# A hybrid decoder step: the pooling stage with feature-major rows, one ordered load queue, a norm centred on four tiles, and activation rows of 272 floats

## The chip, the cores and the metric

One core of one Trainium2 chip. The metric is the device time of one execution in microseconds (us). Lower is better.

## What is computed

One step of a small decoder trunk, for a prompt (1 x 256 tokens) and a sample group (8 x 1 token) that share all weights; both stand side by side as 264 columns. The model width is 2048.

```python
# layer 0: pooling mixer; layer 1: gated linear attention (GLA)
for i in range(2):
    x = layer_norm(ALPHA * x + mixer_i(x), ...)
    x = layer_norm(ALPHA * x + sq_relu(x @ w1[i] + b1[i]) @ w2[i] + b2[i], ...)   # w1: 2048 x 8192

# pooling mixer, four groups of 512 channels, windows w = 2, 4, 8, 16
p = trailing_mean(x_group, w) - x_group          # samples: over 15 stored rows and the new one
y = concat_g(p_g @ w_group[g]) * pool_scale
```

The outputs are the two results y, the new pooling states (npp, nps: the last 15 input rows) and the new GLA states. All is float32.

## The kernel before, in words

Activations lie feature-major: a tile is 128 features x 264 columns, and x is 16 such tiles. Each big product is made in three passes, from a high part (`hh`, in the fp32r format) and a low part (`hl`) of x, and a high and a low part of the weight (`whi`, `wlo`): `mm3` issues hh x whi, hl x whi, hh x wlo. One **unit** is a weight block of 2048 x 128 (1 MB, `raw`): 48 matmuls into one bank `ps`. The whole program has 320 units: 128 for each MLP, 48 for the GLA inputs, 16 for the GLA output. `stage` loads a unit, casts its two halves on ACT (`whi`, L133) and subtracts on DVE (`wlo`, L134); `next_unit` stages two units ahead.

The halves of x are kept in `Parts`, two tiles to a pair: `[P, 2, NX]` with NX = 266 (264 columns and two for the norm's gain and bias). The second tile of a pair so starts 1064 bytes behind the first, and a pair takes 2128 bytes (the allocator gives it 2144).

The **pooling stage** comes first. `load(g)` brings a group's band matrix (the pooling weights over time), its input rows token-major (`xt`: two prompt halves and one tile of sample rows) and its weights (`pw`). `pooled(g, tiles)` makes for each tile the pooled rows px by four matmuls with the band (L755 to L758), turns the input to feature-major by three transposes (L764), and writes ALPHA * x to the residual tile `Z[m]` on ACT (L765, L766). `pool_products(g)` makes 16 plain float32 matmuls (L774), and `ln.add` adds each result to Z (L211).

`Norm` follows as tiles arrive. After the first 8 tiles it makes a provisional mean over them (`centre`, L224), and subtracts it from each tile (L232 in `shift`, L237 in `catch_up`). `gather` then makes the tile's hh and hl (L246, L247) and the sum of squares (L253, L255). So MLP units start before the norm is known: the two spare columns carry what corrects a product afterwards (`settle`, L322 to L324), and `stats` (the sums L266 to L273, then `rsqrt`) comes in the midst of unit 0.

PE's order is that of the program text. The orders of ACT, DVE, POOL and of the DMA queues are made by a scheduler when the program is built, and each engine then runs its own list strictly in that order.

Of the kernel before, what the change touches and what calls it, by code (L numbers as in the profile page):

```python
# [6 lines left out]
F32 = mybir.dt.float32  # L7
# [6 lines left out]
P = 128  # L14
# [4 lines left out]
N = NP + NS  # L19
NX = N + 2  # L20
DFF = 8192
NBLK = DFF // D
# [7 lines left out]
ALPHA = 4 ** 0.25  # L30
WARM = 18
PACE_A = (3, 3)
# [19 lines left out]
def _body(ctx, tc, nc, a, o, stop):  # L52
# [18 lines left out]
    ident = keep.tile([P, P], F32, name="ident")  # L71
    epst = keep.tile([P, 1], F32, name="epst")
    lnr = keep.tile([P, N], F32, name="lnr")
# [12 lines left out]
    class Parts:  # L86
# [93 lines left out]

    def rsqrt(out, v, y0, t):
        S.activation(y0, v, AF.Abs_reciprocal_sqrt, bias=epst)
        V.scalar_tensor_tensor(t, y0, -0.5, y0, ALU.mult, ALU.mult)
        V.scalar_tensor_tensor(t, v, EPS, t, ALU.add, ALU.mult)
        V.scalar_tensor_tensor(out, t, 1.5, y0, ALU.add, ALU.mult)
# [4 lines left out]
    class Norm:  # L190
        def __init__(self, name, x, ahead=1):
# [3 lines left out]
            self.shifted = 8  # L195
            self.n = 0
            self.met = 0
            self.done = 0
            self.sd, self.sq, self.c = lnm, lnq, lnr
            if x is not None:  # L200
                at = OFF[self.g]
                gb = par[:, at:at + 2 * KT].rearrange("p (c m) -> p m c", c=2)
                for m in range(0, KT, 2):
                    hi, lo = x.pair(m)
                    G.tensor_copy(hi[:, :, N:], gb[:, m:m + 2])
                    G.tensor_tensor(lo[:, :, N:], gb[:, m:m + 2], hi[:, :, N:].bitcast(F32), op=ALU.subtract)

        def add(self, ps, scale=1.0):
            m = self.n
            self.n += 1  # L210
            V.scalar_tensor_tensor(Z[m], ps[:, :N], scale, Z[m], ALU.mult, ALU.add)  # L211
            if m == 1:
                V.tensor_tensor(self.sd, Z[0], Z[1], op=ALU.add)
            elif 1 < m < 8:
                V.tensor_tensor(self.sd, self.sd, Z[m], op=ALU.add)
            if m == 7:
                later(1, self.centre)
            if m >= 8:
                self.gather(m)
                self.shift(m + 1 + self.ahead)  # L220

        def centre(self):
            cp = bank("ma")[:, :N]
            PE.matmul(cp, lhsT=ones, rhs=self.sd, start=True, stop=True)  # L224
            S.mul(self.c, cp, 1.0 / 1024)
            self.shift(8 + self.ahead)
            background.append(self.catch_up())
# [7 lines left out]
        def catch_up(self):  # L235
            for t in range(8):
                V.tensor_tensor(Z[t], Z[t], self.c, op=ALU.subtract)  # L237
                self.gather(t)
                yield
                if self.ahead:  # L240
                    yield

        def gather(self, t):
# [7 lines left out]
            else:  # L251
# [4 lines left out]
                else:  # L256
                    self.last = sq
            if t == 9:
                V.tensor_tensor(self.sd, Z[8], Z[9], op=ALU.add)
            elif 9 < t < KT - 1:  # L260
                V.tensor_tensor(self.sd, self.sd, Z[t], op=ALU.add)
# [7 lines left out]
        def close_sums(self):  # L269
            assert self.met == KT  # L270
            p1, p2 = self.p1, self.p2
            PE.matmul(p1, lhsT=ones, rhs=Z[KT - 1], start=False, stop=True)
            PE.matmul(p2, lhsT=ones, rhs=self.last, start=False, stop=True)  # L273
            t, v, y0 = wtile(), wtile(), wtile()
            S.activation(t, p1, AF.Square, scale=1.0 / D)
            S.mul(lnm, p1, 1.0 / D)
            V.scalar_tensor_tensor(v, p2, 1.0 / D, t, ALU.mult, ALU.subtract)
            rsqrt(lnr, v, y0, t)

# [78 lines left out]
    def gla(gctx, norm, xp, x, hg):  # L358
# [65 lines left out]
        class Head:  # L424
            def __init__(self, h):
# [294 lines left out]
        for h in range(HEADS):  # L720
            for t in range(4):
# [3 lines left out]
                if t == 0:  # L725
                    for e in range(2):
                        gated.fresh(2 * h + e, gp.tile([P, 2, NX], F32R, name="kq"[e] + "0") if h == 0 else None)
                heads[h].gate(t, ps, gated)
        assert not background and not pending
        return gated  # L730


    xs = Parts("a")
    with tc.tile_pool(name="poolp", bufs=2) as pp:
        band, xt = {}, {}

        pw, px = {}, {}

        def load(g):
            pw[g] = pp.tile([P, D], F32, name="pw", bufs=3)  # L740
            xt[g] = pp.tile([P, 3, 4 * P], F32, name="xt")
            band[g] = pp.tile([P, 280], F32, name="band")
            nc.sync.dma_start(band[g], a["band"][g])
            for t in range(4 if g == 0 else 1):
                c = slice(t * P, t * P + P) if g == 0 else slice(0, 4 * P)
                nc.sync.dma_start(xt[g][:, :, c], a["xt"][g][:, :, c])  # L746
            nc.sync.dma_start(pw[g], a["pw"][g])

        def pooled(g, tiles):
            x, w = xt[g], band[g]  # L750
            for t in tiles:
                c = slice(t * P, t * P + P)
# [12 lines left out]
                S.mul(Z[m][:, :NP], tp[:, :NP], ALPHA)  # L765
                S.mul(Z[m][:, NP:], tp[:, 3 * P - NS:3 * P], ALPHA)  # L766

        def pool_products(g):
            w = pw.pop(g)
            for mt in range(4):  # L770
# [4 lines left out]
                slot()  # L775
                ln.add(ps, prm("pool_scale", 4 * g + mt))

        S.preload_act_table(AF.Abs_reciprocal_sqrt)
        nc.sync.dma_start(ident, a["ident"])
        nc.scalar.dma_start(par, a["par"])  # L780
        V.memset(ones, 1.0)
        V.memset(epst, EPS)
        warm = bank("ma")
        for e in range(WARM):
            PE.matmul(warm[:, :P], lhsT=ones, rhs=ones, start=True, stop=True)
        load(0)
        load(1)
        pooled(0, range(4))
        ln = Norm("mix_0", xs, 0)
        for g in range(4):  # L790
            if g < 3:
                pooled(g + 1, (0,))
            pool_products(g)
            if g < 3:
                pooled(g + 1, (1,))
                slot()
                pooled(g + 1, (2, 3))
            if g < 2:
                load(g + 2)
            if g:  # L800
                stage()
    nc.gpsimd.dma_start(o["npp"], a["xtail"])
    nc.gpsimd.dma_start(o["nps"], a["nps_src"])

# [31 lines left out]
def layout(i):  # L836
# [4 lines left out]
    sp = i["state_pool"][0]  # L841
    rows = np.concatenate([xp, sp.reshape(NS * CTX, D), xs])
    r["xt"] = c(rows.reshape(3, P, 4, 4 * P).transpose(2, 1, 0, 3))
    band = np.zeros((4, P, 280), np.float32)
    for g, w in enumerate(WINDOWS):
# [6 lines left out]
        band[g, :, 144:272] = full[P:, P:]  # L852
        for b in range(NS):
            band[g, (b + 1) * CTX - (w - 1):(b + 1) * CTX, 272 + b] = np.float32(1.0 / w)
            band[g, NS * CTX + b, 272 + b] = np.float32(1.0 / w - 1.0)
    r["band"] = band
# [67 lines left out]
```

## Time and profile before

| | |
|---|---|
| time, median of 3 runs | 2081.34 us (2079.74 to 2082.94) |
| the profiled execution's own time | 2082.59 us |
| its span | 2080.8 us |
| mean granted TensorE clock | 0.995 |
| PE busy | 2055.9 us (99%), 16436 matmul records |
| DVE, ACT busy | 1254.3 us (60%), 1082.0 us (52%) |

The span is the time from the first to the last instruction in the profile; the time holds what lies around it (1.8 us here). PE is busy all but about 25 us. A matmul's end is modelled, and matmuls overlap, so busy time doesn't say how fast PE works: for that one counts matmuls over a stretch.

### The profile page before, as it was taken

What the parts mean: (1) busy time and instruction counts of PE and PEld (TensorE: products, weight loads), DVE (VectorE), ACT (ScalarE), POOL (GpSimd) and SP (SyncE); (2) the same over time, 40 slices, a digit from 0 to 9 for tenths busy, and PEclk for the clock granted to TensorE, in tenths of its full rate; (3) what the DMA queues carried; (4) which work ended last, traced back from release to release, by engine and by line L of the source; (5) the groups of instructions that cost most, each with busy time, mean ns of one, the idle gap of its engine ahead of it and who ended that gap; (6) DMA issues with size and microseconds to landing.
All of it is one profiled execution on the core that took longest, in us unless ns stands there. A gap on an engine that the chain in (4) does not pass through costs nothing.

```text
span 2080.8 us, 38806 instructions
## 1 busy us (share of the span) xinstructions
PE 2055.9 (99%) x16436; PEld 2018.4 (97%) x16436; DVE 1254.3 (60%) x1969; ACT 1082.0 (52%) x1650; POOL 54.9 (3%) x130
## 2 busy tenths in 40 slices
PE   8999999999999999999999999999999999999996
PEld 8999999999999999998899999999999999999996
DVE  3976444444444458986778758865444444444465
ACT  3657355345435545856656645566454345435543
POOL 0000000000000000011111010000000000000000
PEclk9999999999999999999999999999999999999998
DMA  6554555554455554477676444545555455554442
GB/s 239 193 186 175 175 180 183 183 177 175 177 182 183 182 175 171 153 253 256 237 267 237 161 172 175 178 171 180 182 183 180 174 176 180 183 182 177 174 177 83
DMA packets 67470, 386.19 MB, mean 186 GB/s; under 512 B 7808, under 2 KB 12160, under 8 KB 25808
## 3 DMA queue, kind: packets, MB, share of 16 engines
q1 hardware_dynamic: 61232, 363.28, 49.9%
q0 software_dynamic: 5920, 20.28, 2.6%
q8 instruction: 128, 2.10, 0.4%
q14 instruction: 46, 0.38, 0.1%
q10 hardware_dynamic: 144, 0.16, 0.0%
HBM read 362.65 MB, written 22.14 MB: 185 GB/s over the span
## 4 chain that ended last, share of the span: by engine, by line
PE 94%; DVE 3%; ACT 1%; DMA 1%; SPq 0%; issue 0%; ACTq 0%; DVEq 0%
PE ps L146 30%; PE ps L148 30%; PE ps L147 30%; PE ma L469 1%; DVE wlo L134 1%; PE mb L638 1%; PE ma L567 1%; DMA xt<-in_xt 0%; PE ps L774 0%; ACT whi L133 0%; PE mc L624 0%; DMA raw<-in_w 0%; PE ma L523 0%; SPq L746 0%; DMA s<-in_st 0%
## 5 line engine op out<-in xcount | busy, mean ns | idle before, releaser
L147 PE MATMUL ps<-hl,whi 128*128 128x264 f32 (+1 forms) x5120 | 1460.7, 285 | 0.0
L146 PE MATMUL ps<-hh,whi 128*128 128x264 f32 (+1 forms) x5056 | 1454.0, 288 | 0.0
L148 PE MATMUL ps<-hh,wlo 128*128 128x264 f32 (+1 forms) x5056 | 1443.1, 285 | 0.0
L134 DVE TENSOR_TENSOR wlo<-raw,whi 128x1024 fp32r<-128x1024 f32 x640 | 783.5, 1224 | 606.9 <-ACT whi L133 604.6
L133 ACT CAST whi<-raw 128x1024 fp32r<-128x1024 f32 x640 | 671.0, 1049 | 857.9 <-PE ps L147 832.6
L147 PEld LDWEIGHTS ps<-hl,whi 128*128 128x128 f32 x5120 | 968.7, 189 | 3.7 <-issue 1.4
L146 PEld LDWEIGHTS ps<-hh,whi 128*128 128x128 f32 x5056 | 953.7, 189 | 16.5 <-issue 15.8
L148 PEld LDWEIGHTS ps<-hh,wlo 128*128 128x128 f32 x5056 | 955.4, 189 | 0.0
L179 DVE TENSOR_TENSOR hl<-wt,hh 128x264 fp32r<-128x264 f32 x188 | 79.9, 431 | 15.5 <-ACT hh L178 9.8
L350 DVE TENSOR_TENSOR zt<-zt,ps 128x264 f32<-128x264 f32 x96 | 41.2, 429 | 65.7 <-PE ps L148 65.6
L178 ACT CAST hh<-wt 128x264 fp32r<-128x264 f32 x188 | 76.7, 410 | 7.4 <-DVE wt L661 3.2
L339 ACT ACTIVATE wt<-wt 128x264 f32<-128x264 f32 x128 | 54.4, 425 | 3.9
L627 DVE SCALAR_TENSOR_TENSOR s<-mc,k,s 128x512 f32<-128x512 f32 x64 | 45.8, 744 | 3.4 <-PE mc L624 3.4
L338 ACT ACTIVATE wt<-ps,par 128x264 f32<-128x264 f32 x96 | 45.6, 475 | 0.0
L211 DVE SCALAR_TENSOR_TENSOR zt<-ps,zt 128x264 f32<-128x264 f32 x48 | 20.7, 431 | 38.9 <-PE ps L148 38.9
L607 ACT ACTIVATE s<-s,sa 128x512 f32<-128x512 f32 x64 | 42.7, 713 | 2.6 <-DMA s<-in_st 2.6
L628 POOL DMA_DIRECT2D out_ngs<-s x64 | 34.7, 542 | 351.0 <-DVE s L627 343.3
L253 ACT ACTIVATE wt<-zt 128x264 f32<-128x264 f32 x60 | 23.4, 411 | 17.0 <-DVE zt L211 17.0
L774 PE MATMUL ps<-px,pw 128*128 128x264 f32 x128 | 30.9, 402 | 0.0
L774 PEld LDWEIGHTS ps<-px,pw 128*128 128x128 f32 x128 | 25.3, 200 | 4.4
L302 ACT ACTIVATE wt<-zt,par 128x264 f32<-128x264 f32 x48 | 27.4, 601 | 1.1 <-DVE zt L301 1.1
L246 ACT ACTIVATE hh<-zt,par 128x264 fp32r<-128x264 f32 x48 | 24.1, 511 | 5.6 <-DVE zt L237 3.6
(181 smaller groups left out, 897.3 us busy)
## 6 DMA issues: line engine op xcount, KB each, us to landing
raw<-in_w SPq DMA_DIRECT2D x256, 1024.0 KB, 4.8
raw<-in_win SPq DMA_DIRECT2D x48, 1024.0 KB, 5.0
s<-in_st SPq DMA_DIRECT2D x64, 256.0 KB, 5.5
out_ngs<-s POOLq DMA_DIRECT2D x64, 256.0 KB, 3.0
raw<-in_wout SPq DMA_DIRECT2D x16, 1024.0 KB, 4.8
pw<-in_pw SPq DMA_DIRECT2D x4, 1024.0 KB, 9.9
xt<-in_xt SPq DMA_DIRECT2D x3, 768.0 KB, 8.8
out_y<-zt SPq DMA_DIRECT2D x8, 264.0 KB, 2.2
```

The costliest lines, as they stand in the source:

```text
L133: S.copy(hi, src)
L134: V.tensor_tensor(lo, src, hi.bitcast(F32), op=ALU.subtract)
L146: PE.matmul(ps, lhsT=whi, rhs=xh, start=start, stop=False)
L147: PE.matmul(ps, lhsT=whi, rhs=xl, start=False, stop=False)
L148: PE.matmul(ps, lhsT=wlo, rhs=xh, start=False, stop=stop_)
L178: S.copy(x.hi[m][:, :N], src)
L179: V.tensor_tensor(x.lo[m][:, :N], src, x.hi[m][:, :N].bitcast(F32), op=ALU.subtract)
L338: S.activation(t, project(x)[:, :N], AF.Relu, bias=bias)
L339: S.activation(t, t, AF.Square)
L607: S.mul(s0s[b][hf], s0s[b][hf], sa[:, 2 * h + hf, b:b + 1])
L627: V.scalar_tensor_tensor(s0, vb, self.k[:, hf, NP + b:NP + b + 1], s0, ALU.mult, ALU.add)
L774: PE.matmul(ps[:, :N], lhsT=w[:, c], rhs=px[2 * g + k // 2][:, k % 2], start=k == 0, stop=k == 3)
```

## The change

- The prompt rows for the band matmuls come in one DMA per group (two for group 0), the sample rows in a new array `sw`, feature-major; the pooled sample columns are made on DVE (`sampled`) in place of matmuls. The residual rows come feature-major from a new array `xf` right into Z, in place of transposes and ACT copies. The residual is x and not ALPHA * x; pool_scale is divided by ALPHA (`psc`), and the norm's epsilon is halved (ALPHA squared is 2).
- All loads go on SP's queue, three groups at once at the start, `par` among them; `ident` comes later. The two state copies npp and nps go out in the first MLP unit, nps on SP's queue.
- `Norm` for this layer centres on 4 tiles (`first=4`) in place of 8. 18 warming matmuls become 10.
- Pairs of hh and hl are `[P, 2, 272]`: rows of 1088 bytes, pairs of 2176. The matmuls still read 264 or 266 columns.

```diff
+NROW = 272
-WARM = 18
+WARM = 10
...
             if th is None:
-                th = hslot(self.s, i, [P, 2, NX], F32R, "hh")
-            tl = hslot(self.s, 8 + i, [P, 2, NX], F32R, "hl")
+                th = hslot(self.s, i, [P, 2, NROW], F32R, "hh")
+            tl = hslot(self.s, 8 + i, [P, 2, NROW], F32R, "hl")
             self.pairs[i] = th, tl
             for e in range(2):
-                self.hi[2 * i + e], self.lo[2 * i + e] = th[:, e], tl[:, e]
+                self.hi[2 * i + e], self.lo[2 * i + e] = th[:, e, :NX], tl[:, e, :NX]
...
-            if m == 7:
+            if m == self.first - 1:
                 later(1, self.centre)
-            if m >= 8:
+            if m >= self.first:
                 self.gather(m)
                 self.shift(m + 1 + self.ahead)
...
+            if l == 0 and b == 0:
+                nc.gpsimd.dma_start(o["npp"], a["xtail"])
+                nc.sync.dma_start(o["nps"], a["nps_src"])
...
-                    self.k = gp.tile([P, 2, N], F32, name="k0")
-                    self.q = gp.tile([P, 2, N], F32, name="q0")
+                    self.k = gp.tile([P, 2, NROW], F32, name="k0")[:, :, :N]
+                    self.q = gp.tile([P, 2, NROW], F32, name="q0")[:, :, :N]
...
         def load(g):
             pw[g] = pp.tile([P, D], F32, name="pw", bufs=3)
-            xt[g] = pp.tile([P, 3, 4 * P], F32, name="xt")
-            band[g] = pp.tile([P, 280], F32, name="band")
+            xt[g] = pp.tile([P, 4, 2, P], F32, name="xt", bufs=3)
+            band[g] = pp.tile([P, 272], F32, name="band", bufs=3)
             nc.sync.dma_start(band[g], a["band"][g])
-            for t in range(4 if g == 0 else 1):
-                c = slice(t * P, t * P + P) if g == 0 else slice(0, 4 * P)
-                nc.sync.dma_start(xt[g][:, :, c], a["xt"][g][:, :, c])
+            if g == 0:
+                for t in range(0, 4, 2):
+                    nc.sync.dma_start(xt[g][:, t:t + 2], a["xt"][g][:, t:t + 2])
+                nc.sync.dma_start(sw, a["sw"])
+                nc.sync.dma_start(par, a["par"])
+            else:
+                nc.sync.dma_start(xt[g], a["xt"][g])
             nc.sync.dma_start(pw[g], a["pw"][g])
+            nc.sync.dma_start(ZT[:, 4 * g:4 * g + 4], a["xf"][g])
+
+        def sampled(g):
+            w = WINDOWS[g]
+            s = pp.tile([P, 4, NS], F32, name="ws")
+            if w == 2:
+                V.tensor_tensor(s, win[g][:, :, :, 0], win[g][:, :, :, 1], op=ALU.add)
+            else:
+                V.tensor_reduce(s, win[g], axis=mybir.AxisListType.X, op=ALU.add)
+            for i in range(2):
+                px[2 * g + i] = hslot("b", 2 * g + i, [P, 2, N], F32, "px")
+                V.scalar_tensor_tensor(px[2 * g + i][:, :, NP:], s[:, 2 * i:2 * i + 2], 1.0 / w,
+                                       win[g][:, 2 * i:2 * i + 2, :, w - 1], ALU.mult, ALU.subtract)
...
-                ps = bank("ma")[:, :N]
-                PE.matmul(ps[:, :P], lhsT=x[:, 0, c], rhs=w[:, :P], start=True, stop=True)
-                PE.matmul(ps[:, P:NP], lhsT=x[:, 1, c], rhs=w[:, 144:272], start=True, stop=False)
-                PE.matmul(ps[:, P:P + 16], lhsT=x[:, 0, c], rhs=w[:, P:144], start=False, stop=True)
-                PE.matmul(ps[:, NP:], lhsT=x[:, 2, c], rhs=w[:, 272:], start=True, stop=True)
-                if t % 2 == 0:
-                    px[m // 2] = hslot("b", m // 2, [P, 2, N], F32, "px")
-                S.copy(px[m // 2][:, t % 2], ps)
-                tp = bank("mb" if t % 2 else "mc")
-                for e in range(3):
-                    PE.transpose(tp[:, e * P:e * P + P], x[:, e, c], ident)
-                S.mul(Z[m][:, :NP], tp[:, :NP], ALPHA)
-                S.mul(Z[m][:, NP:], tp[:, 3 * P - NS:3 * P], ALPHA)
+                ps = bank("mb" if t % 2 else "mc")[:, :NP]
+                PE.matmul(ps[:, :144], lhsT=x[:, t, 0], rhs=w[:, :144], start=True, stop=False, skip_group_check=True)
+                PE.matmul(ps[:, P:], lhsT=x[:, t, 1], rhs=w[:, 144:], start=False, stop=True, skip_group_check=True)
+                S.copy(px[m // 2][:, t % 2, :NP], ps)
...
-        load(0)
-        load(1)
+        for g in range(3):
+            load(g)
+        sampled(0)
         pooled(0, range(4))
-        ln = Norm("mix_0", xs, 0)
+        V.tensor_scalar(psc, par[:, OFF["pool_scale"]:OFF["pool_scale"] + KT], 1.0 / ALPHA, None, ALU.mult)
+        ln = Norm("mix_0", xs, 0, half=True, first=4)
...
-            if g:
+            if g == 1:
+                nc.sync.dma_start(ident, a["ident"])
+            if g in (1, 2):
                 stage()
```

`pool_products` now also calls `pooled(g + 1, ...)` behind its second, third and fourth result. `stage` is called for two units in the pooling stage, where it was called for three; the third unit is staged when unit 0's product begins.

The scheduler's lists change with it. First ACT, around the first MLP units before: raw_702 is the weight of unit 2 (the third), wt_693 and wt_762 are the results of units 0 and 1 on their way to the MLP's inner activation.

```order
L133 CAST whi_704<-raw_702 128x1024
L246 ACTIVATE hh_100<-zt_85,par_78 128x264
L253 ACTIVATE wt_595<-zt_85 128x264
L275 ACTIVATE wt_657<-ma_651 128x264
L276 ACTIVATE lnm_83<-ma_651 128x264
L182 ACTIVATE wt_659<-wt_658,epst_81 128x264
L133 CAST whi_708<-raw_702 128x1024
L133 CAST whi_773<-raw_771 128x1024
L335 ACTIVATE wt_693<-wt_693,col_692 128x264
L339 ACTIVATE wt_693<-wt_693 128x264
L178 CAST hh_610<-wt_693 128x264
L133 CAST whi_777<-raw_771 128x1024
```

Unit 2's two casts, and the first of unit 3's, stand ahead of unit 0's result (L335).

ACT at the same place now: raw_501 is the weight of unit 2, raw_587 that of unit 3, wt_578 and wt_647 the results of units 0 and 1.

```order
L277 ACTIVATE wt_542<-ma_536 128x264
L278 ACTIVATE lnm_83<-ma_536 128x264
L183 ACTIVATE wt_544<-wt_543,epst_81 128x264
L337 ACTIVATE wt_578<-wt_578,col_577 128x264
L341 ACTIVATE wt_578<-wt_578 128x264
L179 CAST hh_485<-wt_578 128x264
L337 ACTIVATE wt_647<-wt_647,col_646 128x264
L341 ACTIVATE wt_647<-wt_647 128x264
L179 CAST hh_485<-wt_647 128x264
L134 CAST whi_503<-raw_501 128x1024
L134 CAST whi_507<-raw_501 128x1024
L134 CAST whi_589<-raw_587 128x1024
```

Unit 2's two casts now stand behind the result of unit 1 (its last row is the CAST of hh_485 from wt_647).

DVE at this place now, from the step that corrects unit 1's result (wt_647) to the low part of unit 2's weight (wlo_504). The rows L302 and L303 are the norm being applied to Z.

```order
L326 SCALAR_TENSOR_TENSOR wt_647<-lnm_83,col_646,wt_647 128x264
L303 TENSOR_TENSOR zt_85<-zt_85,lnm_83 128x264
L302 TENSOR_TENSOR zt_85<-zt_85,lnr_82 128x264 x2
L303 TENSOR_TENSOR zt_85<-zt_85,lnm_83 128x264 x2
L180 TENSOR_TENSOR hl_486<-wt_647,hh_485 128x264
L302 TENSOR_TENSOR zt_85<-zt_85,lnr_82 128x264 x2
L303 TENSOR_TENSOR zt_85<-zt_85,lnm_83 128x264 x2
L302 TENSOR_TENSOR zt_85<-zt_85,lnr_82 128x264 x2
L303 TENSOR_TENSOR zt_85<-zt_85,lnm_83 128x264 x2
L302 TENSOR_TENSOR zt_85<-zt_85,lnr_82 128x264 x2
L135 TENSOR_TENSOR wlo_504<-raw_501,whi_503 128x1024
```

Ten steps of L302 and L303 now stand between the low part of unit 1's result (L180) and unit 2's first `wlo`.

## Rows read from the trace of the kernel before

**Rows 1.** The page, parts 1 and 4: busy us, shares, and the last chain.

```profile
PE 2055.9 (99%) x16436; PEld 2018.4 (97%) x16436; DVE 1254.3 (60%) x1969; ACT 1082.0 (52%) x1650; POOL 54.9 (3%) x130
...
PE 94%; DVE 3%; ACT 1%; DMA 1%; SPq 0%; issue 0%; ACTq 0%; DVEq 0%
```

**Rows 2.** Groups by line and shape, PE, 161.6 to 822.4 us: count, busy, mean ns.

```profile
L146 PE MATMUL ps<-hh,whi 128*128 128x264 f32 x1792 | 511.3, 285 | 0.0
L148 PE MATMUL ps<-hh,wlo 128*128 128x264 f32 x1792 | 511.3, 285 | 0.0
L147 PE MATMUL ps<-hl,whi 128*128 128x264 f32 x1792 | 510.9, 285 | 0.0
```

**Rows 3.** Timeline, PE, unit of the first MLP: start us, length us, instruction.

```profile
397.58 0.28 PE L147 MATMUL ps<-hl,whi 128*128 128x264 f32 x1
397.70 0.28 PE L148 MATMUL ps<-hh,wlo 128*128 128x264 f32 x1
...
397.94 0.29 PE L147 MATMUL ps<-hl,whi 128*128 128x264 f32 x1
398.07 0.28 PE L148 MATMUL ps<-hh,wlo 128*128 128x264 f32 x1
```

**Rows 4.** Timeline, pooling stage, PE and the queues (idle before, releaser, in brackets).

```profile
1.05 7.04 PE L785 MATMUL ma<-ones 128*128 128x128 f32 x36 [1.05 <-DVE epst L782]
...
1.66 5.13 SPq L746 DMA_DIRECT2D xt<-in_xt  x4
1.93 0.50 POOL L803 DMA_DIRECT2D out_nps<-in_nps_src  x1
...
6.83 1.80 SPq L747 DMA_DIRECT2D pw<-in_pw  x1
...
18.10 0.76 PE L755 MATMUL ma<-band,xt 128*128 128x128 f32 x2 [3.63 <-DMA xt<-in_xt]
...
20.47 9.00 PE L774 MATMUL ps<-px,pw 128*128 128x264 f32 x32
...
31.65 0.39 PE L755 MATMUL ma<-band,xt 128*128 128x128 f32 x2
31.87 0.39 PE L756 MATMUL ma<-band,xt 128*128 128x128 f32 x2
...
34.00 7.29 PE L774 MATMUL ps<-px,pw 128*128 128x264 f32 x32
```

**Rows 5.** Timeline: PE's first MLP matmul.

```profile
64.03 0.48 PE L146 MATMUL ps<-hh,whi 128*128 128x266 f32 x1
```

**Rows 6.** Stretches: length, busy (x) of PE, PEld, DVE, ACT, POOL, granted clock, DMA, GB/s.

```profile
6.87:17.10 10.23, 6.16 (x55) 5.75 (x54) 0.00 (x0) 3.33 (x12) 0.00 (x0) 1.00 0.95 324
17.10:23.93 6.83, 5.83 (x19) 5.10 (x20) 0.00 (x0) 0.83 (x3) 0.00 (x0) 0.50 1.02 420
23.93:64.00 40.07, 40.07 (x243) 35.93 (x242) 29.08 (x67) 23.78 (x66) 0.00 (x0) 1.00 0.37 141
```

**Rows 7.** Timeline, DVE and ACT around the results of the first MLP units.

```profile
79.61 0.15 DVE L322 TENSOR_SCALAR col<-ps 128x2 f32<-128x2 f32 x1
...
80.94 0.52 ACT L335 ACTIVATE wt<-wt,col 128x264 f32<-128x264 f32 x1 [0.77 <-DVE wt L324]
...
81.95 0.41 ACT L178 CAST hh<-wt 128x264 fp32r<-128x264 f32 x1
```

**Rows 8.** The same timeline by engine: ACT's next cast, and DVE's later steps.

```profile
82.27 1.05 ACT L133 CAST whi<-raw 128x1024 fp32r<-128x1024 f32 x1
...
82.40 0.43 DVE L179 TENSOR_TENSOR hl<-wt,hh 128x264 fp32r<-128x264 f32 x1
...
83.09 0.77 DVE L300 TENSOR_TENSOR zt<-zt,lnr 128x264 f32<-128x264 f32 x2
83.78 1.22 DVE L134 TENSOR_TENSOR wlo<-raw,whi 128x1024 fp32r<-128x1024 f32 x1
```

More of the change, by code (lines that the diff above doesn't have):

```diff
@@ L71, in _body @@
     ident = keep.tile([P, P], F32, name="ident")
-    epst = keep.tile([P, 1], F32, name="epst")
+    epst = keep.tile([P, 2], F32, name="epst")
     lnr = keep.tile([P, N], F32, name="lnr")
@@ L179, in split, with rsqrt, __init__ @@
         V.tensor_tensor(x.lo[m][:, :N], src, x.hi[m][:, :N].bitcast(F32), op=ALU.subtract)
-    def rsqrt(out, v, y0, t):
-        S.activation(y0, v, AF.Abs_reciprocal_sqrt, bias=epst)
+    def rsqrt(out, v, y0, t, half=False):
+        S.activation(y0, v, AF.Abs_reciprocal_sqrt, bias=epst[:, half:half + 1])
         V.scalar_tensor_tensor(t, y0, -0.5, y0, ALU.mult, ALU.mult)
-        V.scalar_tensor_tensor(t, v, EPS, t, ALU.add, ALU.mult)
+        V.scalar_tensor_tensor(t, v, EPS / 2 if half else EPS, t, ALU.add, ALU.mult)
         V.scalar_tensor_tensor(out, t, 1.5, y0, ALU.add, ALU.mult)
     class Norm:
-        def __init__(self, name, x, ahead=1):
+        def __init__(self, name, x, ahead=1, half=False, first=8):
+            self.half, self.first = half, first
             self.g, self.b = name.replace("_", "_g"), name.replace("_", "_b")
@@ L194, in __init__ @@
             self.ahead = ahead
-            self.shifted = 8
+            self.shifted = first
             self.n = 0
@@ L224, in centre @@
             PE.matmul(cp, lhsT=ones, rhs=self.sd, start=True, stop=True)
-            S.mul(self.c, cp, 1.0 / 1024)
-            self.shift(8 + self.ahead)
+            S.mul(self.c, cp, 1.0 / (P * self.first))
+            self.shift(self.first + self.ahead)
             background.append(self.catch_up())
@@ L235, in catch_up @@
         def catch_up(self):
-            for t in range(8):
+            for t in range(self.first):
                 V.tensor_tensor(Z[t], Z[t], self.c, op=ALU.subtract)
@@ L257, in gather @@
                     self.last = sq
-            if t == 9:
-                V.tensor_tensor(self.sd, Z[8], Z[9], op=ALU.add)
-            elif 9 < t < KT - 1:
+            if t == self.first + 1:
+                V.tensor_tensor(self.sd, Z[t - 1], Z[t], op=ALU.add)
+            elif self.first + 1 < t < KT - 1:
                 V.tensor_tensor(self.sd, self.sd, Z[t], op=ALU.add)
@@ L277, in close_sums @@
             V.scalar_tensor_tensor(v, p2, 1.0 / D, t, ALU.mult, ALU.subtract)
-            rsqrt(lnr, v, y0, t)
+            rsqrt(lnr, v, y0, t, self.half)
         def stats(self):
@@ L726, in gla @@
                     for e in range(2):
-                        gated.fresh(2 * h + e, gp.tile([P, 2, NX], F32R, name="kq"[e] + "0") if h == 0 else None)
+                        gated.fresh(2 * h + e, gp.tile([P, 2, NROW], F32R, name="kq"[e] + "0") if h == 0 else None)
                 heads[h].gate(t, ps, gated)
@@ L775, in pool_products @@
                 slot()
-                ln.add(ps, prm("pool_scale", 4 * g + mt))
+                ln.add(ps, psc[:, 4 * g + mt:4 * g + mt + 1])
+                if g < 3:
+                    pooled(g + 1, ((), (0,), (1,), (2, 3))[mt])
         S.preload_act_table(AF.Abs_reciprocal_sqrt)
-        nc.sync.dma_start(ident, a["ident"])
-        nc.scalar.dma_start(par, a["par"])
         V.memset(ones, 1.0)
-        V.memset(epst, EPS)
+        V.memset(epst[:, :1], EPS)
+        V.memset(epst[:, 1:], EPS / 2)
         warm = bank("ma")
@@ L841, in layout @@
     sp = i["state_pool"][0]
-    rows = np.concatenate([xp, sp.reshape(NS * CTX, D), xs])
-    r["xt"] = c(rows.reshape(3, P, 4, 4 * P).transpose(2, 1, 0, 3))
-    band = np.zeros((4, P, 280), np.float32)
+    r["xt"] = c(xp.reshape(2, P, 4, 4, P).transpose(2, 1, 3, 0, 4))
+    r["xf"] = c(np.concatenate([xp, xs]).T.reshape(4, 4, P, N).transpose(0, 2, 1, 3))
+    rows = np.concatenate([sp, xs[:, None]], axis=1).reshape(NS, CTX + 1, 4, 4, P)
+    r["sw"] = np.concatenate([c(rows[:, -w:, g].transpose(3, 2, 0, 1)).reshape(P, -1) for g, w in enumerate(WINDOWS)], axis=1)
+    band = np.zeros((4, P, 272), np.float32)
     for g, w in enumerate(WINDOWS):
@@ L852, in layout @@
         band[g, :, 144:272] = full[P:, P:]
-        for b in range(NS):
-            band[g, (b + 1) * CTX - (w - 1):(b + 1) * CTX, 272 + b] = np.float32(1.0 / w)
-            band[g, NS * CTX + b, 272 + b] = np.float32(1.0 / w - 1.0)
     r["band"] = band
```

31 lines of the change are left out of this document (16 added, 15 removed).

## The prediction

> **What bounds the kernel now.** I first read the page: PE is busy 99% of the span, and 94% of the chain that ended last lies on it [rows 1]. No other engine is near that, so time changes only where PE works faster, does less, or waits. The question is then how fast PE works, and where it waits.
>
> For the speed I counted matmuls over a long stretch of the first MLP, where the groups by line show no wait ahead of PE: 3 x 1792 matmuls in the 660.8 us from 161.6 to 822.4 us [rows 2], 122.9 ns each. [...] The whole program has 320 units of 48, so 15,360 such matmuls and 1887 us: one nanosecond on each is 15.4 us.
>
> For the waits I read the pooling stage in the timeline. PE's first MLP matmul starts at 64.03 us [rows 5]. Ahead of it the warming matmuls run from 1.05 to 8.09, the group products take 9.00 us once and then 7.29 us, and PE waits 3.63 us for group 1's rows at 18.10 [rows 4]. [...] From 23.93 on PE is busy throughout: this stage is bound by PE too, after a late start.
>
> **The pooling stage, shorter.** The first product needs band, both halves of xt, sw, par and pw of group 0: 136 + 512 + 480 + 158 + 1024 KB = 2.37 MB, first in SP's queue. At the 420 GB/s of the loaded stretch [rows 6] that is 5.6 us. Before, the first xt was issued at 1.66, behind it pw at 6.83, and the nps copy ran on POOL's queue from 1.93 [rows 4]. With the first issue near 0.75, 1.5 us until bytes flow and about 1 us to land, the first product starts at about 9.0 us; 8 to 11 are the bounds (the lower without the landing, the upper with the rate of 324 GB/s that the first stretch had [rows 6]). It was 20.47.
>
> From there PE does 64 product matmuls at 7.29 / 16 = 0.456 us, 29.2 us; 12 pooled tiles of two matmuls each. The 128-column one takes 0.22 us (start to start, 31.65 to 31.87 [rows 4]), the 144-column one then 0.25, so 5.6 us; and the centre, as long as one product, 0.5. That ends at 44.3 us where it was 64.03: **19.7 us earlier**. The transposes, the small matmuls and the sample matmuls are in that difference, since they stood between the products on PE.
>
> What hides the rest. DVE does five steps a tile for the norm (about 0.37 us each, as in the pairs of L300 that take 0.77 [rows 8]), 16 x 5 x 0.37 = 29.6 us, four `wlo` of 1.14 (4.6 us) and the sample sums (about 2 us): 36 us in the 35 that PE takes, from 9 to 44. It is nearly full, but its last tiles are needed only by the later matmuls of unit 0; I take 0 to 2 us of wait and put 0 into the sum. ACT loses the transposes' copies. The nps copy now stands on SP's queue ahead of unit 2's weight; unit 2 waits longer for something else, next. Ten warming matmuls in place of 18 (7.04 / 18 = 0.39 us each) end at 5; if the clock then rises later than before (it was full from 6.87 on, the row's start), two or three microseconds at half cost up to 1.5 us; nought in the sum.
>
> **A new wait behind it.** ACT's list has the casts of unit 2's weight behind unit 1's result, where before they stood ahead of unit 0's. So PE finishes unit 1, and only then do they start. From the step that reads the result, L322 at 79.61, to the start of L335 1.33 us pass, from there to the end of L178 1.42 (82.36) [rows 7], then the cast takes 1.05 [rows 8]: 3.8 us. DVE in the meantime does L179 (82.40, about 0.4 us) and ten L300/L301 steps at 0.385 (0.77 a pair), then the first `wlo` of 1.22 [rows 8]: 82.4 + 0.4 + 3.9 + 1.2 = 87.9, that is 8.3 us after the result was read. PE can run two matmuls with the high part before that (0.25). I take a wait of **8.0 us**, in two pieces, with 6 and 9 as bounds. What queues behind it: nothing more, as the casts of unit 3 follow directly and have 5.9 us of unit 2 to hide in. But the clock falls: 3.63 us of waiting was enough at 17.10, and it cost 2.9 us. I add **2.9 us** (bounds 1.5 and 3.5). Net of the stage: 19.7 - 8.0 - 2.9 = **8.8 us gained**.
>
> **Rows of 272 floats.** This touches every one of the 15,360 matmuls. In the program before, tile addresses are known: pairs stand 2144 bytes apart and the second tile 1064 further, so a matmul's moving operand starts at 0, 8, 32 or 40 bytes past a multiple of 64 (4416, 3264, 3264 and 4416 of them). With 1088 and 2176 all start at a multiple of 64. Does that matter? I sorted the trace's start-to-start times by these four places, only for the middle matmul (hl) where the one before and the one after have the same place: 120.6 ns at 0 (608 of them), 123.0 at 8 (624), 122.6 at 32 (624), 124.9 at 40 (608). The timeline shows one of each end: 397.58 to 397.70 at place 0, 397.94 to 398.07 at place 40 [rows 3]; only the mean over hundreds resolves less than its 10 ns. Weighted by their counts the four give 122.8, which is the measured pace, so the places explain it as a sum. By modelled ends place 0 has 121.6 instead of 120.6. I take 121.1 for aligned rows: 1.8 ns less, x 15,360 = **27 us gained**. [...] The row that it is nearest to is place 0's own.
>
> [...]
>
> **The sum.** The profiled execution's own time is 2082.59 us, 1.25 above the median of the runs. 2082.59 - 8.8 - 27 = 2046.8; from the median 2045.5. I say **2047 us**.
>
> **Rivals.**
> 1. *Rows of 272 change nothing* and only the stage gains: the sorted means rest on few places (four to five different matmuls each), and might be made by the weights' addresses. 2081.3 - 8.8 = **2072.5**. Chance 0.22.
> 2. *The wait at unit 2 doesn't come or is hidden*, with the pace as forecast: 2081.3 - 19.7 - 27 = **2034.6**. Against it stands the order in which ACT must work. Chance 0.10.
> 3. [...] Chance 0.03.
> 4. *Slower*: place 0 was cheap for where it lay against the weights, and with all moving rows and all weights at multiples of 64 every matmul meets the load of the next weight. At 124.9 ns that is 31 us on the whole program, 2081.3 - 8.8 + 31 = **2104**. It decides from 0.57 ns a matmul on, where it eats the stage's 8.8 us. Chance 0.06.
>
> The forecast itself has 0.59: 2037 (pace 120.6, shorter wait) to 2058 (a gain of 1 ns).
>
> **Range and chances.** A measurement of this kernel tells 0.2% (4.2 us) from no change. To leave out no more than 2 in 10, the range takes the forecast, rival 1, and most of rival 2: 2033 to 2075. Faster by over 0.2%: the forecast, rivals 1 (but for 0.03, where the wait is longer than I price it), 2 and 3: 0.91. Slower: 0.06 from rival 4, less 0.01. Within 0.2%: the remaining 0.04.
>
> **What would show it.** Right: the first MLP matmul near 44 us; a wait of PE of some 8 us in two pieces between units 1 and 2 (about 59 to 68 us), released by ACT's `whi` and DVE's `wlo`, the granted clock at half behind it; units of 5.81 us in place of 5.90, the count of matmuls over 660 us risen from 5376 to some 5450. Wrong: the same count (rival 1) or a lower one (rival 4); a first product later than 11 us, which would mean that the loads and not PE bound the stage; new waits at each group for xf or pw, or a DVE that is late for unit 0.

## The result and the profile after

The changed kernel takes **2056.14 us** (median of 4 runs, 2054.62 to 2058.76), the kernel before 2082.14 us (2079.74 to 2084.03) beside it: a ratio of 0.9874, 95% interval 0.9862 to 0.9886, that is 26 us or 1.3% faster. The profiled execution has a span of 2055.0 us.

The page after, parts 1 and 4, which answer to [rows 1]:

```profile
PE 2022.8 (98%) x16308; PEld 1985.2 (97%) x16308; DVE 1255.5 (61%) x1983; ACT 1077.8 (52%) x1618; POOL 54.8 (3%) x129
...
PE 94%; DVE 4%; DMA 1%; ACT 1%; issue 0%; SPq 0%; ACTq 0%; POOL 0%; DVEq 0%
```

PE is still the bound. Its busy time is 33 us less, and DVE has gone from 3% to 4% of the chain. The groups by line of the stretch from 161.6 to 822.4 us, as in [rows 2]:

```profile
L147 PE MATMUL ps<-hh,whi 128*128 128x264 f32 (+1 forms) x1811 | 514.8, 284 | 0.0
L148 PE MATMUL ps<-hl,whi 128*128 128x264 f32 (+1 forms) x1811 | 513.6, 284 | 0.0
L149 PE MATMUL ps<-hh,wlo 128*128 128x264 f32 (+1 forms) x1811 | 513.1, 283 | 0.0
```

5433 matmuls stand where 5376 stood (some 30 of each line have 266 columns, since the next layer now begins inside the stretch). The mean length of one, 284 ns after 285, hardly shows it; the count does. Then the waits of PE from 0 to 120 us (in all, times, longest):

```profile
PE ps L147 <- ACT whi L134: 4.5, 1, 4.5
PE ps L792 <- DMA pw<-in_pw: 3.7, 1, 3.7
PE ps L149 <- DVE wlo L135: 3.4, 1, 3.4
PE ma L804 <- DVE epst L801: 1.1, 1, 1.1
PE ma L268 <- DVE lnm L263: 0.9, 1, 0.9
```

Before, but for the same 1.1 us for epst, PE waited for xt alone in the same stretch, twice, the longer wait being the 3.63 us of [rows 4]:

```profile
PE ma L755 <- DMA xt<-in_xt: 5.1, 2, 3.6
```

The timeline of PE now tells where the waits for pw and for unit 2's weight lie, and when the MLP begins:

```profile
10.84 5.49 PE L792 MATMUL ps<-px,pw 128*128 128x264 f32 x16 [3.67 <-DMA pw<-in_pw]
...
47.34 0.48 PE L147 MATMUL ps<-hh,whi 128*128 128x266 f32 x1
...
67.43 0.59 PE L147 MATMUL ps<-hh,whi 128*128 128x266 f32 x1 [4.54 <-ACT whi L134]
...
71.67 0.59 PE L149 MATMUL ps<-hh,wlo 128*128 128x266 f32 x1 [3.42 <-DVE wlo L135]
```

and the windows what they do to the clock (length, PE and PEld busy, DVE, ACT, POOL, granted clock, DMA share, GB/s):

```profile
0.00:11.00 11.00, 6.27 (x37) 5.93 (x38) 2.34 (x16) 2.77 (x5) 3.52 (x21) 1.00 0.81 284
11.00:14.43 3.43, 3.43 (x9) 2.61 (x9) 0.00 (x0) 0.00 (x0) 0.00 (x0) 0.50 1.04 432
14.43:47.30 32.87, 32.75 (x170) 28.55 (x169) 27.52 (x65) 17.75 (x42) 0.00 (x0) 1.00 0.71 286
47.30:65.63 18.33, 14.52 (x106) 13.45 (x104) 17.00 (x52) 6.12 (x16) 1.49 (x4) 1.00 0.34 118
65.63:75.87 10.24, 5.01 (x21) 4.70 (x22) 10.24 (x22) 4.56 (x6) 0.00 (x0) 0.50 0.21 59
```

The profile's records of the clock begin at 4.2 us here, and time ahead of them is shown as 1.00. In these stretches the granted clock is at half (0.50) twice, each time with a wait of PE: from 11.02 us on, just behind the 3.67 us for pw, and from 65.63 on, within the 4.54 us for unit 2's weight. What half means shows in the records of the group products: from 11.24 us on, at 0.50, they start 0.44 us apart, from 14.60 on, at 1.00, 0.22. The MLP starts 16.7 us earlier than before (47.34 against 64.03 [rows 5]), but unit 16, the first of the block's second half, only 4.6 us earlier (157.0 against 161.6): the wait for unit 2's weight and the slow stretch behind it eat the rest. From there to the end of the span the kernel before takes 1919.2 us and this one 1898.1: another 21 us, spread over the units.

### The profile page after: what moved, and what is told of

Same layout as the page of the kernel before. It is cut to its first block, busy times and chain, and to the rows that moved or that the text cites. A ratio compares the mean times of both kernels' runs of the same rounds, so it can differ in the third digit from the quotient of the medians.

```text
span 2055.0 us, 38509 instructions
## 1 busy us (share of the span) xinstructions
PE 2022.8 (98%) x16308; PEld 1985.2 (97%) x16308; DVE 1255.5 (61%) x1983; ACT 1077.8 (52%) x1618; POOL 54.8 (3%) x129
## 4 chain that ended last, share of the span: by engine, by line
PE 94%; DVE 4%; DMA 1%; ACT 1%; issue 0%; SPq 0%; ACTq 0%; POOL 0%; DVEq 0%
PE ps L147 30%; PE ps L148 30%; PE ps L149 30%; PE ma L474 1%; PE mb L643 1%; PE ma L572 1%; DVE wlo L135 1%; PE ps L792 0%; PE mc L629 0%; DMA pw<-in_pw 0%; DVE zt L302 0%; PE ma L528 0%; DMA s<-in_st 0%; DVE zt L303 0%; DMA raw<-in_w 0%
## 5 line engine op out<-in xcount | busy, mean ns | idle before, releaser
L147 PE MATMUL ps<-hh,whi 128*128 128x264 f32 (+1 forms) x5056 | 1449.4, 287 | 4.5 <-ACT whi L134 4.5
L147 PEld LDWEIGHTS ps<-hh,whi 128*128 128x128 f32 x5056 | 952.7, 188 | 21.3 <-issue 15.8
L180 DVE TENSOR_TENSOR hl<-wt,hh 128x264 fp32r<-128x264 f32 x188 | 80.0, 432 | 17.6 <-ACT hh L179 11.7
L179 ACT CAST hh<-wt 128x264 fp32r<-128x264 f32 x188 | 76.9, 412 | 7.5 <-DVE wt L666 3.3
L255 ACT ACTIVATE wt<-zt 128x264 f32<-128x264 f32 x60 | 23.7, 412 | 16.8 <-DVE zt L213 16.7
L304 ACT ACTIVATE wt<-zt,par 128x264 f32<-128x264 f32 x48 | 27.6, 604 | 1.1 <-DVE zt L303 1.1
```

The costliest lines, as they stand in the source:

```text
L147: PE.matmul(ps, lhsT=whi, rhs=xh, start=start, stop=False)
L179: S.copy(x.hi[m][:, :N], src)
L180: V.tensor_tensor(x.lo[m][:, :N], src, x.hi[m][:, :N].bitcast(F32), op=ALU.subtract)
```

## The experiments

Two theories of the gain had to be told apart. **Place**: where a moving row starts modulo 64 bytes sets the matmul's pace, and rows of 272 floats made most of the gain. **Stage**: the rows do nothing by themselves. For the stage, a second question: does the wait at unit 2 come from ACT's list, as predicted, and does taking it away bring its time back?

All twelve runs, each with its own ratio to the kernel before, timed beside it:

| run | time us | ratio, 95% interval |
|---|---|---|
| rows_alone | 2063.14 | 0.9907, 0.9890 to 0.9923 |
| stage_alone | 2076.89 | 0.9973, 0.9962 to 0.9984 |
| place32 | 2065.58 | 0.9919, 0.9904 to 0.9934 |
| off2 | 2085.04 | 1.0015, 1.0005 to 1.0025 |
| wplace32 | 2083.80 | 1.0007, 0.9997 to 1.0017 |
| both32 | 2057.44 | 0.9880, 0.9862 to 0.9898 |
| nps_pin | 2054.14 | 0.9865, 0.9851 to 0.9880 |
| nps_poollate | 2048.32 | 0.9837, 0.9823 to 0.9850 |
| late_warm18 | 2045.60 | 0.9824, 0.9811 to 0.9837 |
| cast_pin | 2044.95 | 0.9820, 0.9806 to 0.9833 |
| cast_first8 | 2052.10 | 0.9852, 0.9839 to 0.9866 |
| keep_busy | 2044.99 | 0.9820, 0.9806 to 0.9833 |

### The two halves of the change, each alone

rows_alone puts the row length alone into the kernel before; stage_alone takes it back out of the changed kernel.

```diff
+NROW = 272
-            tl = hslot(self.s, 8 + i, [P, 2, NX], F32R, "hl")
+            tl = hslot(self.s, 8 + i, [P, 2, NROW], F32R, "hl")
```
```diff
-NROW = 272
+NROW = 266
```

> The kernel before with rows of 272 floats and nothing else. Theory (the place of the moving rows modulo 64 bytes sets the pace of the fp32r matmuls): units of 48 matmuls take 5.81 us in place of 5.90 in most phases, 20 to 22 us are gained, 2060 to 2062. Rival (the stage made all of the 26 us, or both are needed): 2078 to 2084.

> The changed kernel with rows of 266 floats; every engine's order is the same as with 272. Theory: units go back to 5.90 us, only the stage's gain stays, 4 to 6 us below the kernel before, 2076 to 2078. Rival (the rows do nothing): 2056, as the changed kernel.

rows_alone gains 18.6 us, stage_alone 4.8; together 23.4, which agrees with 26 within the intervals (each some 2 to 3 us wide to either side). The rows make about four fifths of the gain. The traces part the two at unit 16: from its start to the end of the span the kernel before takes 1919.2 us and stage_alone 1919.0, rows_alone 1899.9 and the changed kernel 1898.1. L147's (before: L146's) matmuls in one stretch of 630 us show it too (length, PE and PEld busy with their counts, granted clock, DMA share, GB/s); before,

```profile
165.00:795.00 630.00, 487.42 (x1709) 322.01 (x1708) 1.00 0.51 179
```

then the changed kernel,

```profile
165.00:795.00 630.00, 491.87 (x1731) 325.37 (x1732) 1.00 0.52 181
```

rows_alone,

```profile
165.00:795.00 630.00, 491.69 (x1730) 325.31 (x1729) 1.00 0.52 181
```

and stage_alone, where every engine's order is that of the changed kernel and only addresses differ:

```profile
165.00:795.00 630.00, 487.39 (x1709) 322.11 (x1709) 1.00 0.51 179
```

### Which place counts

Four kernels move the rows or the weights of the changed kernel by a few bytes. A small tile ahead of the rows, and one behind them that fills up to 256 bytes, shifts the rows alone (place32); a tile behind the rows shifts the weights alone (wplace32); one ahead of both shifts both (both32). off2 moves the rows by 8 bytes inside their tiles.

```diff
+OFS = 2                                   # off2
...
+    hp.tile([P, 8], F32, name="lead")      # place32, both32
     xs = Parts("a")
...
+    hp.tile([P, 56], F32, name="trail")    # place32; [P, 8] and no lead in wplace32
...
-                self.hi[2 * i + e], self.lo[2 * i + e] = th[:, e, :NX], tl[:, e, :NX]
+                self.hi[2 * i + e], self.lo[2 * i + e] = th[:, e, OFS:OFS + NX], tl[:, e, OFS:OFS + NX]
```

> The changed kernel with the rows of both halves moved on by 32 bytes: all moving operands of the MLPs start 32 bytes past a multiple of 64, the weights stay at multiples of 256. Theory (place sets the pace): 122.6 ns as place 32 had in the kernel before, 12,544 of the 15,360 matmuls lose 1.3 ns, 16 us slower than the changed kernel, 2072. Rival (not the place itself but that all rows stand alike): 2056 within 3 us.

> The changed kernel with all rows moved on by 8 bytes inside their tiles: every moving operand of the MLPs and projections starts 8 bytes past a multiple of 64, rows still 1088 bytes apart. If the place sets the pace: 123.0 ns as place 8 had before, 5.90 us a unit, 2080. If even spacing does it: 5.81 us a unit, 2056. After the run with 32 bytes (units of 5.827 us in half of the phases, 5.884 in the other half): one length a phase between those two, 2060 to 2070.

> The changed kernel with the weights moved on by 32 bytes and the MLPs' rows left at multiples of 64. If only the place of the rows against the weights counts, this is the run with the rows moved by 32 bytes: units of 5.83 and 5.88 us, 2065. If the rows' own place counts: units as in the changed kernel, 2056.

> The changed kernel with rows and weights both moved on by 32 bytes. If it is the place of the rows against the weights that counts: units of 5.81 and 5.79 or 5.89 us as in the changed kernel, 2056. If each has its own place to keep: at least as slow as the run with the weights alone moved (units of 5.97 and 5.86), 2083 or more. If the rows' 32 bytes and the weights' 32 bytes add up: 2093.

The mean length of a unit of 48 matmuls, from the start of a phase's first matmul to that of the next phase's, through 16, in the first MLP (w1 and w2 are the two halves of a block; the first block, with 266 columns, is left out):

```text
kernel        rows at  weights at | b1 w1  b1 w2  b2 w1  b2 w2  b3 w1   us
              (mod 64)  (mod 64)
before        0 8 32 40     0     | 5.894  5.898  5.894  5.898  5.894
stage_alone   0 8 32 40     0     | 5.894  5.898  5.894  5.898  5.894
changed           0         0     | 5.814  5.787  5.814  5.892  5.814
rows_alone        0         0     | 5.814  5.892  5.814  5.787  5.814
place32          32         0     | 5.884  5.827  5.884  5.827  5.884
off2              8         0     | 5.946  5.907  5.947  5.907  5.946
wplace32          0        32     | 5.974  5.864  5.974  5.864  5.974
both32           32        32     | 5.814  5.892  5.814  5.787  5.814
```

off2 loses all that the rows had gained and 29 us against the changed kernel: even spacing alone does nothing. It is slower than all three of its expectations. wplace32 leaves the rows at multiples of 64 and loses 28 us, where 0 or 9 were expected: it isn't the rows' own place either. both32 has none of the MLPs' rows and weights at a multiple of 64, and has the changed kernel's unit lengths to the nanosecond, the two lengths of the w2 phases having changed places. The same stretch of 630 us, wplace32:

```profile
165.00:795.00 630.00, 487.60 (x1704) 321.61 (x1704) 1.00 0.51 178
```

and both32:

```profile
165.00:795.00 630.00, 491.72 (x1729) 325.18 (x1729) 1.00 0.52 181
```

So what counts is how the rows lie **against the weights**: moved together by 32 bytes, the one such move that was tried, they keep the pace. Their distance modulo 64 isn't the rule either. place32 and wplace32 put rows and weights 32 bytes apart, one way and the other, which is the same modulo 64, and their units differ (5.884 and 5.827 us against 5.974 and 5.864). Place as such falls, and so does my expectation of 2072 for place32: it came to 2065.58, since half of its phases run at 5.827.

### The wait at unit 2

The prediction put the late casts down to ACT's order. The trace bears it out: ACT cast that weight long after it was there. In the program text the nps copy stands behind the first 16 units, but it was issued in the pooling stage, at 23.12 us, and landed 13.4 us later. Unit 2's weight was issued next, landed 4.9 us after its issue, at 47.1, and ACT began its casts at 66.34:

```profile
23.12 0.67 SPq L345 DMA_DIRECT2D out_nps<-in_nps_src  x1
42.25 4.89 SPq L128 DMA_DIRECT2D raw<-in_w  x2
...
66.34 1.99 ACT L134 CAST whi<-raw 128x1024 fp32r<-128x1024 f32 x2
```

What made that order? The nps copy stands on SP's queue right ahead of unit 2's weight, and the theory is that the scheduler, which plans by its own times, takes the weight to come late. nps_pin pins the copy behind what is traced ahead of it on SP's queue; nps_poollate sends it from POOL's queue, behind POOL's work for the next norm.

```diff
-                nc.sync.dma_start(o["nps"], a["nps_src"])
+                tc.keep_in_program_order(nc.sync.dma_start(o["nps"], a["nps_src"]))
```
```diff
                 ln = Norm(f"ffn_{l}", nxt() if nxt else None)
+                if l == 0:
+                    tc.keep_in_program_order(nc.gpsimd.dma_start(o["nps"], a["nps_src"]))
```

> The changed kernel with the nps copy pinned on SP's queue behind what the code has traced there before it, so that unit 2's weight is not queued behind it in the scheduler's plan and ACT's list has the casts of units 1 and 2 ahead of unit 0's result. Theory: the 7.9 us wait between units 1 and 2 and the 10.2 us at half clock behind it both go; 7.9 and half of the 10.2 are not all lost today, so 9 to 13 us below the changed kernel, 2043 to 2047. Rival 1: the wait goes but the clock falls for another reason, 2048 to 2050. Rival 2: DVE or ACT is late for unit 1 in its place, 2052 to 2058.

> The changed kernel with the nps copy on POOL's queue, pinned behind POOL's work for the next norm, so that it moves at about 715 us on a queue that carries no weights. Theory: the pinned copy on SP's queue took away the wait between units 1 and 2 (unit 16 began at 143.5 us instead of 157.0) and gave 9.8 us of it back when the weight behind the copy came late; on POOL's queue nothing waits behind it, so the whole 13 us stay: 2042 to 2045. Rival (the copy slows the weights wherever it moves, by bandwidth): 2048 to 2054.

With the pin, both casts of unit 2 and the first of unit 3 stand ahead of the norm's sums in ACT's list, the wait between units 1 and 2 is gone, and unit 16 begins at 143.5 us in place of 157.0. But the run gains only 2 us, and PE waits at another place. SP's queue,

```profile
128.14 0.33 SPq L128 DMA_DIRECT2D raw<-in_w  x1
128.52 0.65 SPq L345 DMA_DIRECT2D out_nps<-in_nps_src  x1
134.06 6.25 SPq L128 DMA_DIRECT2D raw<-in_w  x2
```

PE's waits from 130 to 170 us, of the same kernel,

```profile
PE ps L147 <- ACT whi L134: 5.8, 1, 5.8
PE ps L149 <- DVE wlo L135: 0.5, 1, 0.5
```

and ACT's list there:

```profile
137.65 1.05 ACT L134 CAST whi<-raw 128x1024 fp32r<-128x1024 f32 x1 [1.91 <-PE ps L148]
...
159.42 0.60 ACT L304 ACTIVATE wt<-zt,par 128x264 f32<-128x264 f32 x1
159.93 1.98 ACT L134 CAST whi<-raw 128x1024 fp32r<-128x1024 f32 x2
```

The weight issued at 134.06, right behind the copy, is unit 18's. It didn't come late: it landed 4.8 us after its issue, as the weight ahead of the copy did (4.7). It was cast late. Between 137.65 and 159.93 ACT's list has no cast of a weight but, for the most part, the norm's work on x (L304, L309, L179), at which ACT is busy 14.45 of the 15.70 us from 143.5 to 159.2; the casts start 21 us after the weight landed. That is what happened at unit 2 of the changed kernel, where 19 us lay between: both times the weight right behind the copy has its casts late in ACT's list. So the copy's place harms through the list that the scheduler makes, not on the queue. That the scheduler takes this weight to come late fits both lists; its own times were not looked at. The expectation of nps_poollate, by which the weight behind the copy came late, has this step wrong.

PE waits, with 6.8 us at half clock around it, and unit 16 to unit 32 takes 102.8 us in place of 93.0: 9.8 of the 13.5 us are lost again, 90 us later. On POOL's queue (nps_poollate) no such wait comes, PE waits at no weight from 45 to 800 us, and 7.8 us are gained on the changed kernel; 11 to 14 were expected. What was left out of that expectation: in nps_pin the clock had stayed up at the first product, which began at 10.08 us (its first 16 records took 3.64 us, those of a later group, from 19.98 on, 3.56). Here it began at 11.24 and the clock fell, for 3.4 us (10.87 to 14.28), so unit 16 begins at 146.3 and not at 143.5.

### What then bounds the stage

late_warm18 is nps_poollate with `WARM = 18`. cast_pin then pins the casts of unit 2, and cast_first8 takes the centre on eight tiles again. keep_busy puts six more warming matmuls behind the first pooled tiles of cast_pin.

```diff
-WARM = 10
+WARM = 18                                          # late_warm18 and after
...
-            S.copy(hi, src)
+            cast = S.copy(hi, src)
+            if u == 2:                                  # cast_pin
+                tc.keep_in_program_order(cast)
...
-        ln = Norm("mix_0", xs, 0, half=True, first=4)   # cast_first8
+        ln = Norm("mix_0", xs, 0, half=True, first=8)
...
         pooled(0, range(4))
+        for e in range(6):                              # keep_busy
+            PE.matmul(warm[:, :P], lhsT=ones, rhs=ones, start=True, stop=True)
```

> The kernel with the late nps copy and 18 warming matmuls in place of 10. PE's wait ahead of the first product shrinks from 2 to 4 us to under 1.5, since the warming matmuls end about 3 us later and the pooled tiles follow them. Theory: the first product waits for its weight and starts no later, and the clock does not fall behind the wait, up to 1.7 us below the kernel with 10. Rival: the clock stays up there with 10 as well (as it did with the pinned copy on SP's queue), the same time; if the pooled tiles now end after the weight is there, up to 0.5 us above.

> The kernel with the late nps copy and 18 warming matmuls, with ACT's casts of unit 2's weight pinned behind what is traced there before them, so that they no longer stand ahead of the last hh steps of the norm. Theory: in the kernel without the pin ACT waited 5.14 us for unit 2's weight at 42 to 47 us with the last hh steps behind it, DVE waited 2.31 us for those, PE 2.95 us for the sums, and the clock fell for 3.4 us; all of it goes, 3 to 4.5 us below that kernel, 2041 to 2043. Rival (DVE itself is the bound there and is late without ACT's wait too): under 1 us gained, 2044.5 to 2046.

> The kernel with the pinned casts and the centre taken on eight tiles again in place of four. Theory (DVE is as full as PE in this stage, so the centre on four is needed to keep DVE's work in time): the steps of four more tiles wait for the later centre and pile up at the stage's end, PE waits 2 to 4 us at the first sums or in unit 0 and the clock falls behind it: 3 to 9 us above the kernel with four. Rival (DVE has slack enough): within 1.5 us of it.

> The kernel with the pinned casts and six more warming matmuls behind the first pooled tiles, where PE waited 1.72 us for the first product's weight and then ran 3.4 us at half clock. Theory: they fill the wait, the clock stays up, and the first product starts no later than 0.5 us after the weight is there: 1 to 1.7 us below the kernel without them, 2043 to 2044, with the first MLP matmul at 44.5 to 46 us in place of 47.2. Rival (DVE is late for the first sums then, as its work fills the stage): PE waits 2 us or more at the sums instead, the same time within 0.5 us.

late_warm18 gains 2.7 us in the median, more than the 1.7 expected, though its five runs lie between 2044.5 and 2048.0. In the profiled one, near the slow end (2047.81), the clock stays up at the first product (1.00 to 45.3 us) and the MLP starts at 45.3 instead of 47.6. But PE now reaches the norm's sums before DVE is there. The timeline of its PE,

```profile
51.52 0.71 PE L268 MATMUL ma<-lnm,ones 128*128 128x264 f32 x2 [2.95 <-DVE lnm L263]
```

its ACT,

```profile
47.30 1.05 ACT L134 CAST whi<-raw 128x1024 fp32r<-128x1024 f32 x1 [5.14 <-DMA raw<-in_w]
48.25 0.51 ACT L248 ACTIVATE hh<-zt,par 128x264 fp32r<-128x264 f32 x1
```

and its DVE:

```profile
48.79 0.49 DVE L249 SCALAR_TENSOR_TENSOR hl<-zt,par,hh 128x264 fp32r<-128x264 f32 x1 [2.31 <-ACT hh L248]
```

ACT stands at unit 2's cast before the weight is there, and the norm's hh steps queue behind it. With that cast pinned behind them (cast_pin) PE's wait at the sums is 1.0 us, the time 0.65 us less: the rival's size, and no more than the spread of the runs. In its profile the clock fell at the first product again,

```profile
11.13:14.55 3.42, 3.42 (x10) 2.57 (x9) 0.32 (x1) 0.00 (x0) 0.00 (x0) 0.50 1.02 426
```

and the MLP starts at 47.2 in place of 45.3: about half of what the sums gave went there. In keep_busy the clock is full from its first record at 4.3 us through the whole stage, to 46.1 us:

```profile
0.00:11.26 11.26, 9.30 (x64) 8.96 (x65) 2.34 (x16) 2.77 (x5) 3.52 (x21) 1.00 0.81 286
11.26:46.10 34.84, 34.72 (x179) 30.26 (x179) 27.59 (x65) 17.75 (x42) 0.00 (x0) 1.00 0.70 282
```

Its time is that of cast_pin (2044.99 and 2044.95); the 1 to 1.7 us expected don't show. PE's wait at the sums is 0.9 us, so the rival has the time right and its reason wrong. The first product started at 11.26 us in this profile, with 0.91 us of waiting left, and the 1.1 us by which its MLP starts earlier than cast_pin's are within the spread of the runs.

cast_first8 is 7.2 us slower than cast_pin. PE's waits to 60 us:

```profile
PE ps L149 <- DVE zt L215: 2.7, 1, 2.7
PE ma L270 <- DVE lnm L265: 2.0, 1, 2.0
```

and 6.8 us at half clock from 54.0 us on:

```profile
54.00:60.82 6.82, 5.83 (x18) 4.91 (x19) 6.63 (x14) 5.04 (x9) 1.45 (x4) 0.50 0.53 155
```

The centre on four tiles is what lets DVE finish in time, as its theory said.

The best of these, cast_pin and keep_busy, are 37.5 us (1.8%) below the kernel before and 11 us below the changed one, by their ratios 0.982 and 0.9874.

## Why the prediction was right, and where its terms were off

It said 2047 us, in 2033 to 2075, faster; it came to 2056. The stage's path came as foretold and was priced 4 us too well; the rows' term was 6 to 8 us too large, and that it was this near is in part luck. Term by term:

- **First product at 9.0 us (8 to 11): 10.84.** Inside the bounds, near the upper one. The first bytes moved 1.0 us after the first issue, where I took 1.5. The loading was the mis-sized step: from 2.0 us to the landing of pw at 10.7 the rate was 341 GB/s where I took 420, and of the 3.0 MB that had moved by then I had counted 2.37. The bound with 324 was the better guess. For the 1 us to land no run shows a figure of its own; the product began 0.1 us after pw had landed.
- **19.7 us earlier at the first MLP matmul: 16.7.** 1.8 of the 3.0 us are the late first product. The rest is the clock. I priced a later rise behind the ten warming matmuls, "up to 1.5 us", and put nought into the sum. The rise came early: the starts of the warming matmuls' records, 0.21 us apart at first, are 0.11 apart from 4.2 us on, and in the kernel before from 6.8. What came is a fall behind the wait of 3.67 us for pw, for 3.4 us at half; by the 0.44 us between records there and the 0.22 behind it, that is an estimated 1.7 us. I had priced such a fall behind the wait at unit 2 and not here. The work in between was right: 36.5 us from 10.84 to 47.34, less those 1.7, are 34.8, and 35.3 were forecast.
- **A wait of 8.0 us at unit 2 in two pieces: 4.5 and 3.4, 7.9 us**, released by ACT's `whi` and DVE's `wlo` as forecast. nps_pin and nps_poollate show that the lists made it: with the casts moved ahead it is gone, and the weight itself was there 19 us before its cast.
- **2.9 us of clock behind it (1.5 to 3.5):** 10.24 us at half, in which PE worked 5.01; half of that, 2.5 us. The 2.9 is the same estimate for the wait in the pooling stage before: half of the 5.83 us that PE worked while the clock was at 0.50 [rows 6].
- **Stage net 8.8 us: about 5** (4.8 in stage_alone, 4.6 at unit 16). The terms above give 16.7 - 7.9 - 2.5 = 6.3. The rest at unit 16 is the new wait at the norm's sums, 0.9, where I took nought of 0 to 2, and 13 units of 266 columns that became 0.05 us longer each, 0.7.
- **Rows of 272: 27 us forecast, 18.6 in rows_alone, 21 in the changed kernel behind unit 16.** The mechanism was half right: the rows' length does set the pace, but not by their own place. Place modulo 64 was a stand-in for how rows and weights lie to each other, as the weights stood at multiples of 256 throughout. And the sort didn't show that place 0 is cheap. It took only the middle matmul of the three that read a tile. In the trace before, in the w2 phases of the first three blocks of the first MLP, by the places that the prediction gives with [rows 3] (they repeat every four tiles), the three take 124.4, 120.6 and 122.6 ns at place 0, on average 122.5; places 8, 32 and 40 average 122.4, 122.7 and 124.0. That the weighted means gave the measured pace was no test, and that 121.1 ns then came in the w1 phases (5.814 us) is luck. My 1.8 ns a matmul for all 15,360 was too much: it is 1.7 in the w1 phases (5.894 to 5.814), 2.3 in some w2 phases (5.898 to 5.787) and 0.1 in others (5.892), 1.2 over the 64 units of the layer between the MLPs (480.7 to 477.0 us); and the 32 MLP units with 266 columns grew longer, from 5.920 to 5.973 in the first MLP (in rows_alone they stay at 5.920) and from 5.947 to 5.960 in the second.
- **Rivals.** Rival 1 (rows do nothing) falls with rows_alone; rival 2 with the wait seen. Rival 4 had the right pair, rows against weights, and the wrong sign: the rows lay well against them. wplace32 and off2 show what it would have cost: 28 and 29 us, close to the 31 priced. Rival 3 found no sign: the shortest units in the table above take 5.787 us, 120.6 ns a matmul, and no run shows the far faster pace it stood for.

## What to carry to other kernels

When matmuls alternate short moving rows and weight loads, count matmuls over a long stretch, and try a few bytes of padding on either operand: the pace moved here by up to 2.7% (5.814 to 5.974 us a unit) with no instruction changed. A DMA that carries no urgent data still belongs on a queue that carries none: on the weights' queue it put the casts of the weight behind it late in ACT's list, at unit 2 and, pinned later, at unit 18, though the weight was there 19 and 21 us before; on POOL's queue the kernel is 7.8 us faster. So when PE waits for a cast, compare the landing of its weight with the start of the cast before blaming the queue. When a stage is shortened on its bound engine, look at the next one's list before counting the gain: here DVE was busy 27.5 of the 32.9 us, ACT stood 5.14 us at a cast (late_warm18), and the waits on them of 2 us and more (2.95 there, 2.7 and 2.0 in cast_first8) came with the clock at 0.50.

## What was not expected

- Rows and weights don't count symmetrically: rows 32 bytes on with the weights in place, 5.884 and 5.827 us a unit; weights 32 bytes on with the rows in place, 5.974 and 5.864. Why is open; no run looked at the memory's side.
- The same tiles, in the same order on PE, ran at three lengths. In the changed kernel the second halves of blocks 0, 1 and 2 read h from the same place and take 5.814, 5.787 and 5.892 us a unit, steady from the second unit of a phase on; in rows_alone, both32 and nps_poollate they take 5.787, 5.892 and 5.787. In the second MLP, where x lies where h lay in the first, the first halves of blocks 1 and 2 take 5.787, then 5.892, in all of them. A phase seems to fall into one of a few rhythms by the way it begins. That is argued from these lengths alone; no run chose the rhythm, which would be worth 1.7 us a phase.
- The clock at the first product fell behind waits of 3.67 us (the changed kernel), 3.65 us (nps_poollate), 2.23 us (wplace32) and 1.72 us (cast_pin), and not behind 2.24 us (nps_pin) or 1.29 us (late_warm18): the length of the wait alone doesn't decide it. In wplace32, where it was at half from 10.23 to 13.64 us:

```profile
10.66 3.71 PE L792 MATMUL ps<-px,pw 128*128 128x264 f32 x9 [2.23 <-DMA pw<-in_pw]
```
